# Dense scores in a hybrid encoder layer: the second products of two key tiles, 64 rows deep, in the two halves of the rows

## The chip, the cores and the metric

The kernel runs on one core of one Trainium2 chip. The core has a matrix engine (TensorE, PE in the profile, with its loads of weights as PEld), a vector engine (VectorE, DVE), an engine for functions (ScalarE, ACT), a general engine (GpSimd, POOL) and an engine that only issues transfers (SyncE, SP). SBUF, the memory that all of them read, has 128 rows (partitions). A matmul multiplies weights and moving data that both lie along the rows, adds up over the rows, and writes into a bank of the accumulator memory (PSUM). How many rows take part is the depth of the product. The metric is the device time of one execution in microseconds (us); lower is better.

## The reference, cut to what matters

One encoder layer on 1024 tokens with a model width of 1024. An input projection feeds two groups of attention heads: group A is dense, 8 query heads that share 2 key heads, with a norm on queries and keys and a rotary embedding; group B looks through dilated windows. Then come an output projection and a feed-forward part with a convolution. The change touches the dense scores of group A alone:

```python
def global_gqa_attention(q, k, v):
    b, s = q.shape[0], q.shape[1]
    nb = s // Q_BLOCK
    qg = q.reshape(b, nb, Q_BLOCK, N_KV_A, GQA_GROUP, HEAD_DIM).transpose(1, 0, 2, 3, 4, 5)
    scale = HEAD_DIM ** -0.5

    def block(qb):
        sc = jnp.einsum('bqkgd,bskd->bkgqs', qb, k, preferred_element_type=jnp.float32) * scale
        p = jax.nn.softmax(sc, axis=-1)
        return jnp.einsum('bkgqs,bskd->bqkgd', p.astype(v.dtype), v)
```

A head has 64 dimensions, so a score is a product of depth 64. All is float32.

## The kernel before

**Split numbers.** PE takes float32 in a rounded form (fp32r). To keep the precision, the kernel splits a value x into a high part (x rounded to fp32r) and a low part (x less the high part, rounded). A product of queries q and keys k is then high x high + high x low + low x high. With depth 64 two of the three fit into one product of depth 128. The tile that starts at R_K2A holds, for each tile of 128 keys, the low parts of k in rows 0 to 63 and the high parts in rows 64 to 127. The queries' tile q2 (R_Q2A) holds the high parts of q in rows 0 to 63 and the low parts in rows 64 to 127. Their product gives low x high and high x low. A second tile, R_KHA, holds the high parts of k in rows 0 to 63 and zeros below, and its product with q2 gives high x high. The two products add up in one bank.

**The dense stage.** The function a_main_bounded does one group: one block of 128 queries, 4 heads that share a key head, so 512 columns. There are 16 groups. A group has 8 tiles of 128 keys, taken in 4 steps j of two tiles u = 0, 1. In a step PE makes the scores of both tiles in two neighbouring banks (L773 and L774, twice each), ACT takes the exponential of both at once (L779), ACT or DVE rounds it to the high part (L783, L781), and DVE makes the low part (L784). Three steps later PE multiplies with the values (L757, six matmuls of 512 columns for a step). At a group's end DVE copies the result (L767), PE transposes it (L762), and DVE divides by the sum (L803, L804).

**Preparation.** a_prep makes q2 for the next group while the present one runs. Its step nat splits the queries (L665 on ACT, L666 on DVE); its step first transposes them on PE (L192, in the helper tr_r) and lets ACT copy them to q2 (L687). q2 has two buffers, which the groups use in turn. A table in the main loop, plan, tells behind which of the eight key tiles of a group the next of these steps is taken: (0, 1, 0, 0, 1, 0, 0, 0) takes nat behind tile 1 and first behind tile 4, that is in steps j = 0 and j = 2.

**Other work in the stage.** Sums, norms and rotary turns that are left over from the projection are dealt out over the first groups (on POOL L530 and L304, on DVE L537 and L540 among others), and a tick, a small copy (L1323, L558), ties each to the group that it is to run in. Later groups carry the norms of group B's queries, and parts of the next stage's preparation (L849 and L850 split its keys, L838 and L839 its values). Transfers within SBUF go through POOL's queue: k_ready makes R_KHA in that way with four transfers (L354), and the next stage does the same (L880). The engines' queues are in order; a scheduler sets the order of each from the program, so a step can stand earlier or later than the code reads.

Of the kernel before, what the change touches and what calls it, by code (L numbers as in the profile page):

```python
# [45 lines left out]
R_K2A = 16384  # L46
R_KHA = R_K2A + 2048
R_W = R_KHA + 6144
# [26 lines left out]
R_QLN = R_XT + 1024  # L75
R_Q2A = R_XT + 2048
R_QLA = R_XT + 3072
R_PH = R_XT + 4096
R_PL = R_XT + 6144
R_VB = R_XT + 8192  # L80
# [2 lines left out]
R_VA = R_XT + 9248  # L83
R_PHB = (R_PH, R_PH + 1024, R_XT + 1024, R_XT + 13824)
R_PLB = (R_PL, R_PL + 1024, R_XT + 3072, R_XT + 14848)
# [51 lines left out]
def tile_encoder_layer(ctx, tc, x, w_in, gains, outg, norm1_g, norm2_g, w_out, w_up, conv_w, conv_b,  # L137
# [14 lines left out]
    def emit(bounded):  # L152
# [3 lines left out]
        gp = nc.gpsimd  # L156
        mm = nc.tensor.matmul
# [5 lines left out]
        def r(off, n):  # L163
            return bigr[:, off:off + n]
# [20 lines left out]
        def bank(i, n=512, o=0):  # L185
            return PS[:, 512 * i + o:512 * i + o + n]
# [26 lines left out]
        def next_tr():  # L213
            trb[0] ^= 1
            return 4 + trb[0]
# [8 lines left out]
        def qab(tt):  # L224
            return O_QAB + 1024 * tt
# [424 lines left out]
        def p_slots():  # L650
            i = p_n[0]
            p_n[0] += 1
            return p_ring[i % len(p_ring)], R_PH + 512 * (i % 4), R_PL + 512 * (i % 4)

        def q_nat(src, stride, eng, n, o, qln=R_QLN):

            q = fp(src, [stride, n], [1, 64])
            act(rp(R_QD + o, [128, n], [64, 2], [1, 64]), fp(src, [stride, n], [0, 2], [1, 64]), AF.Copy)
            eng.tensor_tensor(rp(qln + o, [128, n], [1, 64]), q, rfp(R_QD + o, [128, n], [1, 64]), op=OP.subtract)


        def q_pair(src, stride, eng, n, o):

            q = fp(src, [stride, n], [1, 64])
            act(rp(R_QD + o, [128, n], [1, 64]), q, AF.Copy)  # L665
            eng.tensor_tensor(rp(R_QD + 64 + o, [128, n], [1, 64]), q, rfp(R_QD + o, [128, n], [1, 64]), op=OP.subtract)  # L666

        def grp(g):
            b, kv = divmod(g, 2)
            return (4 * (g // 8) + g % 4, g // 4 % 2) if bounded else (b, kv)  # L670

        def a_prep(g):
            b, kv = grp(g)
            o = 512 * (g % 2)
            q2 = R_Q2A + 512 * (g % 2)
            ql = R_QLA + 512 * (g % 2)

            def nat():
                if bounded:
                    return q_pair(qab(b) + 256 * kv, 64, vec, 4, o)  # L680
                q_nat(qab(b) + 256 * kv, 64, vec, 4, o)

            def first():
                t = next_tr()
                for i in range(4):
                    tr_r(t, i, r(R_QD + o + 128 * i, 128))
                act(r(q2, 512), bank(t), AF.Copy)  # L687

            def mx(i):
                for hf in range(2):  # L690
                    b = hf
                    mm(bank(b), r(q2 + 128 * i, 128), r(R_K2A + 1024 * kv + 512 * hf, 512), start=True, stop=True)
                    vec.tensor_reduce(f(SM_MC + 8 * hf + i, 1), bank(b), axis=AX.X, op=OP.max)

            def last():
                vec.tensor_tensor(rp(R_QLN + 512 * kv + 64, [128, 4]), f(SM_MC, 4), f(SM_MC + 8, 4), op=OP.max)
                t = next_tr()
                for i in range(4):
                    tr_r(t, i, r(R_QLN + 128 * (4 * kv + i), 128))
                act(r(ql, 512), bank(t), AF.Copy)  # L700

            if bounded:
                return [nat, first]
            return [nat, first] + [lambda i=i: mx(i) for i in range(4)] + [last]

        def a_main(g, prep, tail, late, plan, late_plan):
# [4 lines left out]
            q2 = R_Q2A + 512 * (g % 2)  # L711
            ql = R_QLA + 512 * (g % 2)
            ob = 6 + g % 2
# [29 lines left out]
        def a_main_bounded(g, prep, tail, late, plan, late_plan):  # L743

            b, kv = grp(g)
            b2, kv2 = grp(max(g - 2, 0))
            q2 = R_Q2A + 512 * (g % 2)
            ob = 6 + g % 2
            slots = {}

            def pv(j):
                ph, pl = slots[j]
                for u in range(2):
                    kt = 2 * j + u
                    v = R_VA + 132 * kt + 66 * kv
                    for i, (w, p) in enumerate(((v, ph), (v + 1056, ph), (v, pl))):
                        mm(bank(ob)[0:66], r(w, 66), r(p + 512 * u, 512), start=(kt == 0 and i == 0), stop=(kt == 7 and i == 2))  # L757

            def o_turn():
                t = next_tr()  # L760
                for i in range(4):
                    nc.tensor.transpose(bank(t, 66, 128 * i), f(F_OT + 128 * i, 128)[0:66], f(O_IDF, 66)[0:66])  # L762
                o_norm(t, 128, qab(b) + 256 * kv, ([64, 4], [1, 64]))

            def last():
                pv(3)
                vec.tensor_copy(f(F_OT, 512)[0:66], bank(ob)[0:66])  # L767

            for j in range(4):
                st = 2 * (j % 2)  # L770
                for u in range(2):
                    kt = 2 * j + u
                    mm(bank(st + u), r(R_K2A + 1024 * kv + 128 * kt, 128), r(q2, 512), start=True, stop=False)  # L773
                    mm(bank(st + u), r(R_KHA + 1024 * kv + 128 * kt, 128), r(q2, 512), start=False, stop=True)  # L774
                n = pairs[0]
                pairs[0] += 1
                p, ph, pl = F_PB[n % 3], R_PHB[j], R_PLB[j]
                slots[j] = ph, pl
                act(f(p, 1024), bank(st, 1024), AF.Exp)  # L779
                if j == 1:  # L780
                    vec.tensor_copy(r(ph, 1024), f(p, 1024))  # L781
                else:
                    act(r(ph, 1024), f(p, 1024), AF.Copy)  # L783
                vec.tensor_tensor(r(pl, 1024), f(p, 1024), rf(ph, 1024), op=OP.subtract)  # L784
                for kt in (2 * j, 2 * j + 1):
                    take(prep, plan[kt])
                    take(late, late_plan[kt])
                    now = f(qab(b2) + 256 * kv2, 1) if 0 < kt < 7 and g > 1 else \
                        rf(R_Q2A + 512 * ((g + (kt == 7)) % 2), 1)
                    for step in spread.pop((g, kt), []):  # L790
                        step(now)
                step = tail.pop(0) if tail else None
                if step:
                    step()
                if j > 2:
                    pv(j - 3)

            behind, turn[:] = turn[:], [o_turn]
            return [lambda: [t() for t in [lambda: pv(1)] + behind], lambda: pv(2), last, o_turn if g == 15 else None]
# [189 lines left out]
        def b_p_bounded(h, i):  # L989
            ta, tb = F_TEE[h % 2]  # L990
            st, p = 2 * (i % 2), F_PD[i]
            if not fine(i):
                vec.tensor_tensor(fp(p, [512, 2], [256, 2], [1, 256]), pp(512 * st, [512, 2], [256, 2], [1, 256]),
                                  fp(tb, [0, 2], [128, 2], [1, 256]), op=OP.mult)
                return
            ph, pl = R_PH + 512 * i, R_PL + 512 * i
            vec.tensor_tensor(fp(p, [256, 4], [64, 4], [1, 64]), pp(512 * st, [256, 4], [64, 4], [1, 64]),
# [4 lines left out]
        def b_pv_bounded(h, i):  # L1002
            if fine(i):
                ph, pl = R_PH + 512 * i, R_PL + 512 * i
                for u in range(4):
# [344 lines left out]
        for g in range(16):  # L1350

            prep += a_prep(g + 1) if g < 15 else []
            if g == 14:
                prep += [lambda: b_split(0)] + sum(sum(b_prep(0), []), [])
            plan = {14: (1, 1, 0, 1, 0, 1, 1, 0), 15: (1, 1, 0, 1, 0, 0, 0, 0)}.get(g, (0, 1, 0, 0, 1, 0, 0, 0)) if bounded else {14: (1, 1, 1, 1, 1, 2, 2, 2), 15: (2, 2, 2, 2, 1, 1, 1, 1)}.get(
                g, (1, 1, 1, 1, 1, 1, 1, 0))
            tail = a_main(g, prep, tail, late, plan, (0, 2, 2, 2, 1, 1, 1, 1))
            if g == 7:
                if not bounded:
                    dma(f(F_CNT, 384), cnt)  # L1360
                if not bounded:
                    gp.memset(fp(F_VCN + 64, [66, 8]), 1.0)
                    load_vc(0)
            if g in (4, 7):
                wo_load(g // 7)
            if g == 9:
                load_tee(0, 0)
                load_tee(0, 1)
                load_tmx(1)
            if g == 11:  # L1370
                load_k(0)
            if g == 13:
                load_k(1)
            if g == 10 and bounded:
                load_v(0)
            if g == (12 if bounded else 5):
                v_split(R_VB, F_VBN)
                load_v(1)
            if g > 3 and fills:
                b, kv = grp(g - 2 if bounded else g - 1)  # L1380
                fills.pop(0)(qab(b) + 256 * kv)
# [411 lines left out]
        for m in range(2, len(order)):  # L1793
            j, n = order[m]
# [111 lines left out]
```

## Time and profile before

| | us |
|---|---|
| median of 3 runs (lowest, highest) | 1220.58 (1219.28, 1222.5) |
| the profiled execution | 1221.38 |
| its span in the profile | 1219.6 |
| the dense stage, 16 groups, 207.5 to 364.6 | 157.1 |

The profile shows one execution. A row of the timeline gives the start, the length and what ran; several instructions of the same kind are merged, with their number behind an x. A row of a group of instructions gives the number, the busy time, the mean length in ns, and the idle time before. A matmul's shape stands as rows*columns of the weights, then the moving data. The ends of matmuls are modelled, so their starts are the safer reading. Weights are loaded by an instruction of their own, which can run beside a matmul.

### The profile page before, as it was taken

The page shows a single profiled execution, that of the slowest core. Times are in us where ns is not written, and L with a number is a line of the kernel's source. Part 1 is how long each engine was busy: PE and PEld are TensorE (multiplying, and loading weights), DVE is VectorE, ACT ScalarE, POOL GpSimd, SP SyncE. Part 2 cuts the span into 40 slices and gives each one's busy share as a digit, 9 for nine tenths or more (in the row PEclk, how much of TensorE's full clock was granted, in tenths as well). Part 3 has the DMA queues.
Part 4 walks back from the last instruction along what each step waited for, and adds up shares of the span by engine and source line. Part 5 has one row for each costly group of instructions (what it writes and reads, how often), then busy time and mean ns, then how long its engine had stood idle before and what let it go on. Part 6 is the DMA issues. An engine that isn't in the chain of part 4 may idle for free.

```text
span 1219.6 us, 17814 instructions
## 1 busy us (share of the span) xinstructions
PE 1191.7 (98%) x6615; PEld 1007.2 (83%) x6615; DVE 998.0 (82%) x1324; ACT 674.1 (55%) x976; POOL 398.4 (33%) x307
## 2 busy tenths in 40 slices
PE   7999999999999999999999999999999999999998
PEld 7999999666669997888788888877888788888886
DVE  5988687989988878666999999999999997876673
ACT  7856455889887767436544444445444453543431
POOL 1710122230024530010465666557575644000000
PEclk9999999999999999999999999999999999999999
DMA  8036301020015655232132232322332257977872
GB/s 281 25 103 154 108 18 42 1 57 18 1 30 125 153 117 173 89 102 95 61 112 95 87 113 97 111 95 87 113 112 100 83 184 252 338 239 243 291 233 85
DMA packets 121565, 147.00 MB, mean 121 GB/s; under 512 B 51137, under 2 KB 79617, under 8 KB 121473
## 3 DMA queue, kind: packets, MB, share of 16 engines
q1 hardware_dynamic: 119329, 140.05, 35.9%
q0 software_dynamic: 2144, 5.77, 2.2%
q8 instruction: 53, 0.87, 0.3%
q14 instruction: 39, 0.32, 0.1%
HBM read 107.25 MB, written 33.82 MB: 116 GB/s over the span
## 4 chain that ended last, share of the span: by engine, by line
PE 68%; DVE 17%; issue 5%; ACT 4%; DMA 3%; POOL 1%; SPq 0%; DVEq 0%; ACTq 0%; POOLq 0%
DVE bigf L1603 7%; PE ps L1570 7%; PE ps L1572 6%; PE ps L1571 6%; PE ps L757 6%; PE ps L1704 6%; PE ps L1703 6%; PE ps L1702 6%; DVE bigf L1574 3%; PE ps L1125 2%; PE ps L1126 2%; PE ps L1124 2%; PE ps L434 2%; PE ps L435 2%; PE ps L773 2%
## 5 line engine op out<-in xcount | busy, mean ns | idle before, releaser
L1570 PE MATMUL ps<-bigr 128*128 128x512 f32 x616 | 241.0, 392 | 6.3 <-DVE bigf L1574 5.8
L1571 PE MATMUL ps<-bigr 128*128 128x512 f32 x616 | 239.7, 389 | 0.0
L1572 PE MATMUL ps<-bigr 128*128 128x512 f32 x616 | 239.7, 389 | 0.0
L1603 DVE SCALAR_TENSOR_TENSOR bigf<-bigf 128x768 f32<-128x768 f32 (+1 forms) x176 | 178.7, 1073 | 26.5 <-ACT bigf L1601 26.4
L1553 ACT ACTIVATE bigr<-bigf 128x512 fp32r<-128x512 f32 x154 | 93.2, 625 | 139.5 <-POOL bigf L1545 70.2
L1682 ACT ACTIVATE bigr<-bigf 128x1024 fp32r<-128x1024 f32 (+1 forms) x99 | 83.7, 867 | 115.8 <-PE ps L1704 67.6
L1570 PEld LDWEIGHTS ps<-bigr 128*128 128x128 f32 x616 | 115.6, 188 | 35.0 <-DVE bigf L1574 9.2
L1572 PEld LDWEIGHTS ps<-bigr 128*128 128x128 f32 x616 | 115.6, 188 | 24.1
L1571 PEld LDWEIGHTS ps<-bigr 128*128 128x128 f32 x616 | 115.7, 188 | 23.7
L434 PE MATMUL ps<-bigr 128*128 128x256 f32 x448 | 127.3, 285 | 1.2 <-ACT bigf L310 1.2
L1554 DVE TENSOR_TENSOR bigr<-bigf,bigr 128x512 fp32r<-128x512 f32 x112 | 125.2, 1135 | 3.2 <-ACT bigr L1553 2.5
L435 PE MATMUL ps<-bigr 128*128 128x256 f32 x448 | 126.9, 283 | 0.6 <-DVE bigr L418 0.6
L436 PE MATMUL ps<-bigr 128*128 128x256 f32 x448 | 126.7, 283 | 0.0
L1702 PE MATMUL ps<-bigr 128*128 128x512 f32 x308 | 119.8, 389 | 0.0
L1703 PE MATMUL ps<-bigr 128*128 128x512 f32 x308 | 119.8, 389 | 0.0
L1704 PE MATMUL ps<-bigr 128*128 128x512 f32 x308 | 119.8, 389 | 0.0
L1683 DVE TENSOR_TENSOR bigr<-bigf,bigr 128x1024 fp32r<-128x1024 f32 (+1 forms) x99 | 97.6, 1005 | 24.8 <-ACT bigr L1682 21.4
L757 PE MATMUL ps<-bigr 128*66 128x512 f32 x384 | 99.9, 394 | 0.0
L434 PEld LDWEIGHTS ps<-bigr 128*128 128x128 f32 x448 | 85.8, 192 | 1.8 <-ACT bigf L310 1.5
L435 PEld LDWEIGHTS ps<-bigr 128*128 128x128 f32 x448 | 85.9, 192 | 0.8 <-DVE bigr L418 0.8
L784 DVE TENSOR_TENSOR bigr<-bigf,bigr 128x1024 fp32r<-128x1024 f32 x64 | 80.8, 1269 | 6.4 <-ACT bigr L783 5.7
L436 PEld LDWEIGHTS ps<-bigr 128*128 128x128 f32 x448 | 85.9, 192 | 0.0
(231 smaller groups left out, 2508.8 us busy)
## 6 DMA issues: line engine op xcount, KB each, us to landing
bigf<-w_down SPq DMA_DIRECT2D x99, 256.0 KB, 4.3
bigf<-w_up SPq DMA_DIRECT2D x44, 512.0 KB, 3.6
bigf<-gscr SPq DMA_DIRECT2D x77, 256.0 KB, 4.3
gscr<-bigf SPq DMA_DIRECT2D x31, 512.0 KB, 2.6
bigf<-w_in SPq DMA_DIRECT2D x8, 1024.0 KB, 5.4
bigf<-x SPq DMA_DIRECT2D x15, 512.0 KB, 7.0
bigf<-w_out SPq DMA_DIRECT2D x8, 512.0 KB, 3.9
bigr<-bigr POOLq DMA_DIRECT2D x16, 256.0 KB, 3.8
```

Of the source, the lines that this page charges most:

```text
L434: mm(o, ah, wh, start=(k == 0 and t % 2 == 0 and n != 2), stop=False, skip_group_check=True)
L435: mm(o, ah, wl, start=False, stop=False, skip_group_check=True)
L436: mm(o, al, wh, start=False, stop=(k == 3), skip_group_check=True)
L757: mm(bank(ob)[0:66], r(w, 66), r(p + 512 * u, 512), start=(kt == 0 and i == 0), stop=(kt == 7 and i == 2))
L1554: (gp if n in (2, 4) and m > 3 else vec).tensor_tensor(rp(o + 512, [128, 4], [1, 128]), src, rfp(o, [128, 4], [1, 128]), op=OP.subtract)
L1570: mm(bank(b), wh, th, start=(k == 0 and n in (1, 5, 6, 7)), stop=False, skip_group_check=True)
L1571: mm(bank(b), wh, tl, start=False, stop=False, skip_group_check=True)
L1572: mm(bank(b), wl, th, start=False, stop=(k == 3), skip_group_check=True)
L1603: vec.scalar_tensor_tensor(f(a + o, n), f(i + d, n), w_, f(a + o, n), op0=OP.mult, op1=OP.add)
L1702: mm(o, ah, r(d, 512), start=(q == 0 and n in (1, 5, 2)), stop=False, skip_group_check=True)
L1703: mm(o, ah, r(d + 1024, 512), start=False, stop=False, skip_group_check=True)
L1704: mm(o, al, r(d, 512), start=False, stop=(q == NQ - 1), skip_group_check=True)
```

## The change

Three things are edited, in the dense stage alone.

The second products of a step's two key tiles, which gave high x high at a depth of 128 with zeros in half of the rows, are now 64 rows deep. That of tile u = 0 reads rows 0 to 63 of R_KHA and of q2. That of tile u = 1 reads rows 64 to 127 of R_K2A, where the high parts of its keys lie already, and rows 64 to 127 of a new tile, R_Q3A. The two stand one behind the other, after the two first products. No tile's depth was 64 in the program before.

R_Q3A takes a copy of the queries' high parts, moved from rows 0 to 63 to rows 64 to 127. A transfer on POOL's queue makes it for each group, in the step first behind the copy on ACT. It has two buffers, as q2 has.

The table plan takes first one step earlier, behind tile 2 (j = 1), and in group 14 its entries move.

```diff
+R_Q3A = R_W + 6144
...
                 act(r(q2, 512), bank(t), AF.Copy)
+                if bounded:
+                    gp.dma_start(r(R_Q3A + 512 * (g % 2), 512)[64:128], r(q2, 512)[0:64])
...
                 st = 2 * (j % 2)
+                k2, kh = [o + 1024 * kv + 256 * j for o in (R_K2A, R_KHA)]
                 for u in range(2):
-                    kt = 2 * j + u
-                    mm(bank(st + u), r(R_K2A + 1024 * kv + 128 * kt, 128), r(q2, 512), start=True, stop=False)
-                    mm(bank(st + u), r(R_KHA + 1024 * kv + 128 * kt, 128), r(q2, 512), start=False, stop=True)
+                    mm(bank(st + u), r(k2 + 128 * u, 128), r(q2, 512), start=True, stop=False)
+                mm(bank(st), r(kh, 128)[0:64], r(q2, 512)[0:64], start=False, stop=True)
+                mm(bank(st + 1), r(k2 + 128, 128)[64:128], r(R_Q3A + 512 * (g % 2), 512)[64:128], start=False, stop=True)
...
-            plan = {14: (1, 1, 0, 1, 0, 1, 1, 0), 15: (1, 1, 0, 1, 0, 0, 0, 0)}.get(g, (0, 1, 0, 0, 1, 0, 0, 0)) if bounded else
+            plan = {14: (1, 0, 1, 0, 1, 1, 1, 0), 15: (1, 1, 0, 1, 0, 0, 0, 0)}.get(g, (0, 1, 1, 0, 0, 0, 0, 0)) if bounded else
```

Lines of the changed kernel have other numbers: the first products are L776, the second L777 (u = 0) and L778 (u = 1), the products with the values L760, the transposes of queries L193, of results L765, the copy on ACT L688, the new transfer L690.

PE's queue in one group of the dense stage, from its step j = 1, before:

```order
L773 MATMUL ps<-bigr 128x512
L774 MATMUL ps<-bigr 128x512
L773 MATMUL ps<-bigr 128x512
L774 MATMUL ps<-bigr 128x512
L757 MATMUL ps<-bigr 66x512 x6
L773 MATMUL ps<-bigr 128x512
L774 MATMUL ps<-bigr 128x512
L773 MATMUL ps<-bigr 128x512
L774 MATMUL ps<-bigr 128x512
L192 MATMUL ps<-bigr 128x128 x4
L757 MATMUL ps<-bigr 66x512 x6
```

And the same place now:

```order
L776 MATMUL ps<-bigr 128x512 x2
L777 MATMUL ps<-bigr 128x512
L778 MATMUL ps<-bigr 128x512
L193 MATMUL ps<-bigr 128x128 x4
L760 MATMUL ps<-bigr 66x512 x6
L776 MATMUL ps<-bigr 128x512 x2
L777 MATMUL ps<-bigr 128x512
L778 MATMUL ps<-bigr 128x512
L760 MATMUL ps<-bigr 66x512 x6
```

The two second products now stand together between the two first ones and the six with the values, and the transposes of the next group's queries (L193) stand one step earlier.

POOL's queue from k_ready's transfers through the dense stage, before:

```order
L354 DMA bigr<-bigr 64x2x256 x4
L530 TENSOR_TENSOR bigf<-bigf 128x512
L304 TENSOR_TENSOR bigf<-bigf 128x8x16 x8
L530 TENSOR_TENSOR bigf<-bigf 128x512
L304 TENSOR_TENSOR bigf<-bigf 128x8x16 x8
L530 TENSOR_TENSOR bigf<-bigf 128x512
L304 TENSOR_TENSOR bigf<-bigf 128x8x16 x8
L1452 MEMSET bigf 128x8
L850 TENSOR_TENSOR bigr<-bigf,bigr 128x8x64
L839 TENSOR_TENSOR bigr<-bigf,bigr 128x8x64
```

And now, from the first turns on (L531 and L305 are the table and the turns, L854 and L843 the splits of keys and values):

```order
L305 TENSOR_TENSOR bigf<-bigf 128x8x16 x8
L690 DMA bigr<-bigr 64x512 x3
L531 TENSOR_TENSOR bigf<-bigf 128x512
L305 TENSOR_TENSOR bigf<-bigf 128x8x16 x8
L690 DMA bigr<-bigr 64x512
L531 TENSOR_TENSOR bigf<-bigf 128x512
L305 TENSOR_TENSOR bigf<-bigf 128x8x16 x8
L1456 MEMSET bigf 128x8
L690 DMA bigr<-bigr 64x512
L854 TENSOR_TENSOR bigr<-bigf,bigr 128x8x64
L690 DMA bigr<-bigr 64x512
L843 TENSOR_TENSOR bigr<-bigf,bigr 128x8x64
```

The new transfers stand among the turns and the splits: one ahead of this piece, those of groups 1 to 3 ahead of the second table, that of group 4 ahead of the third, those of groups 5 and 6 behind the last turns, and the other nine behind the split of the values.

More of the change, by code (lines that the diff above doesn't have):

```diff
@@ L1354, in emit @@
                 prep += [lambda: b_split(0)] + sum(sum(b_prep(0), []), [])
-            plan = {14: (1, 1, 0, 1, 0, 1, 1, 0), 15: (1, 1, 0, 1, 0, 0, 0, 0)}.get(g, (0, 1, 0, 0, 1, 0, 0, 0)) if bounded else {14: (1, 1, 1, 1, 1, 2, 2, 2), 15: (2, 2, 2, 2, 1, 1, 1, 1)}.get(
+            plan = {14: (1, 0, 1, 0, 1, 1, 1, 0), 15: (1, 1, 0, 1, 0, 0, 0, 0)}.get(g, (0, 1, 1, 0, 0, 0, 0, 0)) if bounded else {14: (1, 1, 1, 1, 1, 2, 2, 2), 15: (2, 2, 2, 2, 1, 1, 1, 1)}.get(
                 g, (1, 1, 1, 1, 1, 1, 1, 0))
```

## The prediction

> **What bounds the kernel now.** I read the page's busy times first, then the groups of instructions, then the timeline of one group of the dense stage, then the same stage cut at the starts of its sixteen groups.
>
> ```profile
> span 1219.6 us, 17814 instructions
> PE 1191.7 (98%) x6615; PEld 1007.2 (83%) x6615; DVE 998.0 (82%) x1324; ACT 674.1 (55%) x976; POOL 398.4 (33%) x307
> ...
> L773 PE MATMUL ps<-bigr 128*128 128x512 f32 x128 | 51.7, 404 | 0.3 <-ACT bigr L687 0.3
> ...
> L774 PE MATMUL ps<-bigr 128*128 128x512 f32 x128 | 50.3, 393 | 0.0
> ```
>
> L773 and L774 are the two products of the dense scores, 128 of each, and only this stage is edited. A record of 393 ns is not what a matmul costs here. The timeline of PE in one group shows the cost:
>
> ```profile
> 289.07 0.40 PE L774 MATMUL ps<-bigr 128*128 128x512 f32 x1
> 289.30 0.39 PE L773 MATMUL ps<-bigr 128*128 128x512 f32 x1
> 289.53 0.39 PE L774 MATMUL ps<-bigr 128*128 128x512 f32 x1
> ...
> 294.68 1.56 PE L757 MATMUL ps<-bigr 128*66 128x512 f32 x6
> 296.08 0.41 PE L762 MATMUL ps<-bigf 66*128 66x66 f32 x4
> 296.30 0.48 PE L773 MATMUL ps<-bigr 128*128 128x512 f32 x1
> ```
>
> The second column is a record's length, but the starts are 0.23 us apart (289.07, 289.30, 289.53). So 0.23 us is the slot of a matmul, and 0.39 - 0.23 = 0.16 us of each record lies under the next one: two are in flight at once. The weights are loaded ahead, in the slot before:
>
> ```profile
> 288.84 0.19 PEld L774 LDWEIGHTS ps<-bigr 128*128 128x128 f32 x1
> 289.07 0.19 PEld L773 LDWEIGHTS ps<-bigr 128*128 128x128 f32 x1
> ```
>
> The load for the matmul that starts at 289.30 begins at 289.07, so its 0.19 us are hidden. A group has 40 slots, 16 for scores and 24 for L757: 40 x 0.23 = 9.2 us. Two sets of four transposes bring it near 9.8 us. Here is the stage by group (columns: the stretch, its length, then PE, PEld, DVE, ACT and POOL busy, with instructions in brackets, the granted clock, and DMA):
>
> ```profile
> 207.53:213.01 5.48, 5.21 (x29) 3.91 (x27) 3.90 (x5) 4.64 (x7) 0.00 (x0) 1.00 0.00 0
> 213.01:223.31 10.30, 10.30 (x44) 6.93 (x45) 10.30 (x13) 9.55 (x12) 0.00 (x0) 1.00 0.00 0
> 223.31:233.16 9.85, 9.85 (x49) 6.83 (x48) 8.44 (x13) 7.97 (x11) 4.07 (x4) 1.00 0.01 2
> 233.16:243.00 9.84, 9.84 (x50) 6.84 (x48) 9.28 (x13) 7.86 (x10) 3.69 (x6) 1.00 0.00 1
> 243.00:252.87 9.87, 9.87 (x50) 6.85 (x49) 7.37 (x14) 7.89 (x10) 7.25 (x10) 1.00 0.19 47
> 252.87:264.24 11.37, 10.07 (x50) 6.76 (x48) 10.68 (x16) 8.45 (x11) 3.10 (x1) 1.00 0.36 88
> 264.24:274.07 9.83, 9.83 (x50) 6.86 (x49) 9.35 (x17) 9.19 (x13) 1.39 (x1) 1.00 0.11 27
> 274.07:283.93 9.86, 9.86 (x50) 6.79 (x48) 9.80 (x16) 9.76 (x12) 0.00 (x0) 1.00 0.19 53
> 283.93:293.77 9.84, 9.84 (x49) 6.83 (x49) 9.54 (x19) 8.72 (x11) 0.00 (x0) 1.00 0.01 2
> 293.77:303.89 10.12, 10.12 (x50) 6.79 (x48) 9.55 (x16) 9.52 (x13) 0.00 (x0) 1.00 0.00 0
> 303.89:313.61 9.72, 9.72 (x48) 6.81 (x48) 8.92 (x16) 9.68 (x12) 0.00 (x0) 1.00 0.01 2
> 313.61:323.46 9.85, 9.85 (x49) 6.83 (x48) 9.57 (x17) 8.01 (x10) 0.00 (x0) 1.00 0.00 1
> 323.46:333.31 9.85, 9.85 (x49) 6.84 (x48) 9.61 (x15) 7.88 (x9) 0.00 (x0) 1.00 0.00 0
> 333.31:343.13 9.82, 9.82 (x49) 6.86 (x48) 9.72 (x18) 8.32 (x12) 0.00 (x0) 1.00 0.12 28
> 343.13:354.66 11.53, 10.68 (x58) 7.45 (x56) 8.67 (x12) 9.98 (x14) 1.42 (x1) 1.00 0.00 1
> 354.66:364.60 9.94, 9.94 (x53) 7.04 (x52) 7.45 (x8) 9.47 (x13) 4.68 (x5) 1.00 0.28 54
> sum 157.07, PE 154.66 PEld 107.21 DVE 142.13 ACT 136.89 POOL 25.60; mean PE 9.67 PEld 6.70 DVE 8.88 ACT 8.56 POOL 1.60
> ```
>
> PE fills 154.7 of 157.1 us, at full clock (1.00). So the stage is bound by PE, slot after slot, and what a slot costs more or less goes into the time. But DVE (142.1) and ACT (136.9) are close behind, and in the group at 274.07 they are busy 9.80 and 9.76 us of 9.86. A slower PE costs nearly in full, a faster one is soon caught by the other two.
>
> **The change, part by part.** The sum is made against the profiled execution, 1221.4 us (span 1219.6 and 1.8 around it), which is 0.8 above the median of the runs, 1220.6.
>
> *The slots.* Four full-depth slots per step become two full-depth ones and two of 64 rows. The two of 64 rows read different halves of the rows and write different banks, so they can share a slot. No row here shows two matmuls in one slot: the pair costs between 0.23 us (together) and 0.46 (one after the other). I take 0.23, since neither needs anything of the other. With 16 groups of 4 steps, that is 64 pairs x 0.23 = 14.7 us off PE at most.
>
> *The change of depth.* PE now goes from 128 rows to 64 and back in each step, 128 changes in all. No dense slot of before does that. Two rows bound it. From below, L762 above: its 66-row transposes start at 296.08, and the sixth L757 before it started about 294.68 + 5 x 0.23 = 295.83, so another kind of matmul came in after 0.25 us, a slot as usual: cost 0. From above, the only matmul of fewer than 64 rows:
>
> ```profile
> 6.48 0.18 PEld L593 LDWEIGHTS ps<-bigf 8*128 8x128 f32 x1 [0.33 <-issue]
> 6.48 0.27 PE L593 MATMUL ps<-bigf 8*128 8x8 f32 x1
> ```
>
> Its load of weights and its matmul start together, so nothing was loaded ahead. If a change waits until PE is empty and only then loads weights, it costs 0.16 + 0.19 = 0.35 us. I take the step between the ends, 0.16: the matmul in flight ends before the next depth begins, but weights are still loaded ahead. It lies next to the middle of 0 and 0.35. Two changes are then 0.32 us against 0.23 saved, so a step loses 0.32 - 0.23 = 0.09 to 0.10 us, and 64 steps lose about 6.1 us. The ends are -14.7 us on PE and 64 x (0.70 - 0.23) = +30 us.
>
> The Trainium skill speaks against this change at this point: "TensorEngine Tiling (Array Packing)", section "Tiling Modes", says that changing the tiling mode, not just the tile, drains the TensorE. It gives no time for that; by it the sum is on the losing side, +6 us or more, and without it on the winning side. No row of this profile shows a drain, so the trace neither agrees nor disagrees.
>
> *The copy.* Sixteen transfers of 64 x 512 go into POOL's queue. Nearest are the four of L354, as large and within SBUF:
>
> ```profile
> L354 POOL DMA_DIRECT2D bigr<-bigr x4: 578/587/813, 189.2 to 196.7; - x4
> ...
> DMA to landing us min/median/max: 2.3/2.6/3.8
> ```
>
> POOL pays 0.59 us for each, 9.4 us in all, and has 157.1 - 25.6 us free in the stage; that is its cover. PE needs the copy for the fourth product of a group. The transposes of the next group's queries move up one step (ten slots, about 2.4 us), which pays for most of the 2.6 us. Three places are tight. In the first group there is no slack:
>
> ```profile
> 212.35 0.60 ACT L687 ACTIVATE bigr<-ps 128x512 fp32r<-128x512 f32 x1
> ...
> 213.01 0.50 PE L773 MATMUL ps<-bigr 128*128 128x512 f32 x1 [0.27 <-ACT bigr L687]
> ```
>
> L687 moves up by one exponential here and ends near 212.0; the group's first product follows it at once, and its copy lands near 212.0 + 2.6 = 214.6 (from the issue), against a need three slots in, at 212.1 + 0.7 = 212.8. PE would wait 1.8 us, but DVE is busy for all of the next group (10.30 of 10.30), so part is hidden: between 0 and 2 us, I take 1. In the group at 252.87 the transfer stands in POOL's queue behind the turns:
>
> ```profile
> 244.02 2.49 POOL bigf L530
> ...
> 246.58 4.73 POOL bigf L304 x8
> ...
> 251.33 1.23 DVE bigf L537
> ```
>
> This is the chain of waits: POOL is done at 251.3, the copy lands at 253.9, needed at 253.6. That group idles 11.37 - 10.07 = 1.3 us on this chain anyway, so I take nothing. Last, b_split's L850 and v_split's L839 stand between the later transfers; they keep their places, and the copies of groups 6 and 7 wait behind them, with the 2.4 us in hand: 0, at most 1.
>
> *The order.* The moved transposes (L192) are the same work earlier, but they need the split of the queries (L666 on DVE) one step sooner.
>
> ```profile
> 285.85 0.41 DVE L666 TENSOR_TENSOR bigr<-bigf,bigr 128x256 fp32r<-128x256 f32 x1
> ...
> 289.76 0.45 PE L192 MATMUL ps<-bigr 128*128 128x128 f32 x4
> ```
>
> Here it is done 3.5 us ahead (289.76 - 286.26), more than the 2.4 that they move. The other moves on ACT and DVE change places, not work: 0.
>
> *Sum.* +6.1 (depth) + 1 (first copy) - 0.8 (the groups at 252.87 and 343.13 idle 1.3 and 0.85 us on other engines, which covers their 0.4 each) = +6.3 us. From the median: 1220.6 + 6.3 = **1227 us**.
>
> **The rivals.** *A change of depth costs nothing* (faster). Then PE has 0.92 us less to do in a group. What of it can be had is what DVE and ACT leave: for each group the lesser of 0.92 and its length less the busier of DVE and ACT. In the rows above from the third on that is 0.92, 0.56, 0.92, 0.69, 0.48, 0.06, 0.30, 0.57, 0.04, 0.28, 0.24, 0.10, 0.92, 0.47, and nothing in the first two (they wait for L687 and DVE): 6.5 us, so 1214. It ends at 1217 if the chain through POOL keeps the groups at 243.00 and 252.87 (1.6 us) and the first copy is late, and at 1211 if a lead in one group helps the next. For it speaks L762, which slots in without a gap; against it, that L762 keeps the full depth. It decides below 0.11 us a change, where the two changes cost the slot saved. The Trainium skill, "TensorE: Matmul & The Clock Gate", section "Part 3: Packing small matmuls — row/col tiling", says that tiles in different row groups run at once, some 4 ns apart; by that rule alone this rival is the result, and no row here shows it.
>
> *PE empties and the loading is exposed as well* (slower still): 0.35 us a change, 64 x 0.47 = 30 us, less about 2 in the groups that idle: 1248. For it speaks L593; against it, that L593 may have waited for its own data.
>
> *The pair doesn't run together and a change costs nothing*: four slots as before, 1221, with late copies up to 1223. The records would then show the pair 0.23 us apart.
>
> **How the numbers follow.** Forecast 0.43 (its own range 1223 to 1232: 0.14 to 0.2 us a change, first copy 0 to 2), no cost of depth 0.35, exposed loading 0.13, nothing gained 0.09. Within 0.3% (3.7 us) two times cannot be told apart. Slower: 0.40 of the forecast, 0.13, and 0.03 of the last, 0.56. Faster: 0.33 of the first rival. Same: 0.03 + 0.02 + 0.06 = 0.11. The range 1211 to 1246 takes in the first rival and the near part of the second, and leaves out some 0.12.
>
> **What would show it.** In the timeline of PE, the second half's product starts within a few hundredths of the first half's; the first half's product starts 0.39 us (not 0.23) after the last full one, and the first L757 behind the pair 0.39 after it. A group then takes about 10.2 us, and DVE's share of the stage falls. If the group shrinks to 9.5 or less with DVE near 100%, the first rival holds; if the weights' loads of the pair start only after the last full product ends, the second. Waits of PE for the copy should show in the group at 213 alone. The forecast is wrong above all if the array changes its depth as it goes.

## The result, and the profile after

| | before | changed |
|---|---|---|
| median (us) | 1220.92 | 1229.07 |
| lowest to highest | 1219.28 to 1222.5 | 1228.02 to 1229.21 |
| runs | 4 | 4 |
| span of the profiled execution | 1219.6 | 1227.1 |
| dense stage in it, first score to the next stage's first product | 157.2 | 164.5 |

The changed kernel is slower: ratio 1.0062, 95% interval 1.005 to 1.0075. The forecast was 1227. Of the 7.5 us between the spans, 7.3 stand in the dense stage. One execution of two_steps_half below (1461.6 us) and one of the kernel before beside it (1468.4) ran at a granted clock of 0.75 and are left out of the ratios.

The page's busy times and the groups of instructions on PE in the changed kernel (L776 is the first product, L777 and L778 the pair of 64 rows, L760 the products with the values):

```profile
span 1227.1 us, 17854 instructions
PE 1201.3 (98%) x6615; PEld 992.8 (81%) x6615; DVE 998.9 (81%) x1324; ACT 677.0 (55%) x976; POOL 406.8 (33%) x323
...
L760 PE MATMUL ps<-bigr 128*66 128x512 f32 x384 | 102.8, 400 | 0.0
L776 PE MATMUL ps<-bigr 128*128 128x512 f32 x128 | 41.5, 405 | 0.0
L777 PE MATMUL ps<-bigr 64*128 64x512 f32 x64 | 31.7, 496 | 0.0
L778 PE MATMUL ps<-bigr 64*128 64x512 f32 x64 | 31.7, 496 | 0.0
```

PE has as many matmuls as before, and the records of the pair are 496 ns long against 393 for the product that they replace. The timeline of PE shows where a step's time goes:

```profile
287.30 0.63 PE L776 MATMUL ps<-bigr 128*128 128x512 f32 x2
287.86 0.50 PE L777 MATMUL ps<-bigr 64*128 64x512 f32 x1
287.86 0.50 PE L778 MATMUL ps<-bigr 64*128 64x512 f32 x1
288.29 1.60 PE L760 MATMUL ps<-bigr 128*66 128x512 f32 x6
```

And a stretch a little later, in which the second of the two L776 has a row of its own, with the loads of weights:

```profile
290.26 0.40 PE L776 MATMUL ps<-bigr 128*128 128x512 f32 x1
...
290.59 0.18 PEld L777 LDWEIGHTS ps<-bigr 64*128 64x128 f32 x1 [0.37 <-issue]
290.59 0.49 PE L777 MATMUL ps<-bigr 64*128 64x512 f32 x1
290.59 0.18 PEld L778 LDWEIGHTS ps<-bigr 64*128 64x128 f32 x1
290.60 0.50 PE L778 MATMUL ps<-bigr 64*128 64x512 f32 x1
```

Three things are to be seen. The pair does share a slot: its two products start together. The pair starts 0.33 us after the last full product (290.59 - 290.26), where a slot is 0.23. And its weights begin to load only then, at the same moment as the products' records, after 0.37 us in which the loader waited for nothing that the profile names ("issue"). In a plain step of the kernel before, each load ran under the slot ahead of it.

The way back reads alike: L760 follows the pair after 0.43 us (288.29 - 287.86), and six of them last 1.60 us where six lasted 1.54 to 1.56.

The dense stage by group (the columns as in the prediction; four of the sixteen, and the sum):

```profile
213.64:224.92 11.28, 11.28 (x44) 5.96 (x45) 10.69 (x14) 9.99 (x13) 0.51 (x1) 1.00 0.12 23
...
255.84:266.60 10.76, 10.54 (x50) 5.71 (x48) 10.72 (x15) 9.10 (x12) 4.83 (x3) 1.00 0.42 103
...
287.30:297.68 10.38, 10.38 (x49) 5.80 (x48) 8.85 (x17) 9.42 (x11) 0.51 (x1) 1.00 0.07 14
...
349.29:361.88 12.59, 11.25 (x57) 6.41 (x56) 8.06 (x11) 9.86 (x14) 3.15 (x2) 1.00 0.06 10
...
sum 164.48, PE 162.88 PEld 90.78 DVE 143.71 ACT 139.88 POOL 33.97; mean PE 10.18 PEld 5.67 DVE 8.98 ACT 8.74 POOL 2.12
```

A plain group takes 10.3 to 10.4 us instead of 9.85, and DVE and ACT do the same work as before in more time. PE bounds the stage more than it did.

### The profile page after: what moved, and what is told of

The parts are those of the page before. It is cut to its first block, busy times and chain, and to the rows that moved or that the text cites. A ratio compares the mean times of both kernels' runs of the same rounds, so it can differ in the third digit from the quotient of the medians.

```text
span 1227.1 us, 17854 instructions
## 1 busy us (share of the span) xinstructions
PE 1201.3 (98%) x6615; PEld 992.8 (81%) x6615; DVE 998.9 (81%) x1324; ACT 677.0 (55%) x976; POOL 406.8 (33%) x323
## 4 chain that ended last, share of the span: by engine, by line
PE 57%; DVE 19%; issue 13%; ACT 4%; DMA 4%; POOL 2%; SPq 0%; DVEq 0%; POOLq 0%; ACTq 0%
DVE bigf L1607 7%; PE ps L1574 7%; PE ps L1576 6%; PE ps L1575 6%; PE ps L1706 6%; PE ps L1707 6%; PE ps L1708 6%; DVE bigf L1578 2%; PE ps L1128 2%; PE ps L1130 2%; PE ps L1129 2%; PE ps L760 2%; PE ps L990 2%; DVE bigr L1558 2%; PE ps L1023 2%
## 5 line engine op out<-in xcount | busy, mean ns | idle before, releaser
L1687 DVE TENSOR_TENSOR bigr<-bigf,bigr 128x1024 fp32r<-128x1024 f32 (+1 forms) x99 | 96.6, 995 | 23.9 <-ACT bigr L1686 20.6
L760 PE MATMUL ps<-bigr 128*66 128x512 f32 x384 | 102.8, 400 | 0.0
```

## The experiments

Six kernels ran, four on one chip and two on another, each beside the kernel before. The theory: each change between 128 and 64 rows stops PE for a fixed time, and two changes cost more than the slot that the pair saves. The diffs are against the changed kernel where nothing else is said. The rivals: the copy and the moved steps cost the time; the 64-row products are slow in themselves or don't share a slot; the cost goes by the pair and not by the change.

### copy_full_depth: the copy and the order, without the depth

```diff
-                mm(bank(st), r(kh, 128)[0:64], r(q2, 512)[0:64], start=False, stop=True)
-                mm(bank(st + 1), r(k2 + 128, 128)[64:128], r(R_Q3A + 512 * (g % 2), 512)[64:128], start=False, stop=True)
+                for u in range(2):
+                    mm(bank(st + u), r(kh + 128 * u, 128), r(q2, 512), start=False, stop=True)
```

> The changed kernel with its copy, its table and its order, but the two second products at the full depth of 128 again (the copy is made and not read). If the change of depth is the cost, this stands near the kernel before: 1221 to 1222.5 us, and a dense group takes 9.8 us again. If the copy and the moved steps are the cost, it stands near the changed kernel, 1228 to 1229, with groups of 10.3.

Measured: 1222.25 us against 1221.15 before, ratio 1.0008 (0.9999 to 1.0017). The whole dense stage in one window, and a step of it:

```profile
207.31:365.69 158.38, 154.76 (x757) 107.44 (x756) 142.90 (x212) 138.82 (x166) 35.79 (x42) 1.00 0.15 32
```

```profile
291.56 0.62 PE L776 MATMUL ps<-bigr 128*128 128x512 f32 x2
292.01 0.62 PE L778 MATMUL ps<-bigr 128*128 128x512 f32 x2
292.46 1.53 PE L760 MATMUL ps<-bigr 128*66 128x512 f32 x6
```

Four slots from 291.56 to 292.46, 0.23 each again. The sixteen transfers, the moved transposes and the changed orders of ACT and DVE cost the stage 1.2 us (158.4 against 157.2), and the change of depth the rest. The 1.2 us are all idle time of PE (158.38 - 154.76 = 3.6 us, where the kernel before has 2.4); over the executions the interval takes in no difference at all. What this run can't hold is a wait of PE for the copy, since nothing reads it.

### same_half: both products of 64 rows in the lower half, no copy

```diff
-                if bounded:
-                    gp.dma_start(r(R_Q3A + 512 * (g % 2), 512)[64:128], r(q2, 512)[0:64])
...
-                mm(bank(st), r(kh, 128)[0:64], r(q2, 512)[0:64], start=False, stop=True)
-                mm(bank(st + 1), r(k2 + 128, 128)[64:128], r(R_Q3A + 512 * (g % 2), 512)[64:128], start=False, stop=True)
+                for u in range(2):
+                    mm(bank(st + u), r(kh + 128 * u, 128)[0:64], r(q2, 512)[0:64], start=False, stop=True)
```

> Both second products 64 rows deep, but both in the lower half of the rows, and no copy. If the two halves share a slot in the changed kernel and each step pays 0.35 us for two changes of depth, this one pays the 0.35 without the shared slot: 64 x 0.35 = 22 us over the kernel before, 1242 (1239 to 1245), and the second half-depth product starts 0.23 us after the first. If the halves share nothing, or 64-row products are slow in themselves, it stands with the changed kernel at 1229.

Measured: 1241.78 us, ratio 1.0169 (1.0154 to 1.0184). The timeline of a step:

```profile
290.20 0.63 PE L774 MATMUL ps<-bigr 128*128 128x512 f32 x2
290.76 0.73 PE L776 MATMUL ps<-bigr 64*128 64x512 f32 x2
291.42 1.62 PE L758 MATMUL ps<-bigr 128*66 128x512 f32 x6
```

The two half-depth products now take 0.66 us from start to start of what follows (290.76 to 291.42), against 0.43 for the pair in two halves: the difference is one slot of 0.23. So the halves do share a slot in the changed kernel, and this sharing, less what the copy costs, is worth 1241.8 - 1229.1 = 12.7 us. The cost of the depth is what eats it: without the sharing, 20.6 us over the kernel before, 0.32 us a step. One expectation failed: the second product starts 0.34 us after the first (0.73 less a record of 0.39), not 0.23.

```profile
207.33:385.14 177.81, 176.91 (x756) 97.88 (x755) 143.84 (x212) 140.98 (x166) 26.10 (x27) 1.00 0.07 18
```

In the dense stage PE was busy for 22.2 us more than before (176.91 - 154.66), which is 0.35 us a step, and its idle time fell from 2.4 to 0.9 us. So the two changes cost PE 0.35, as expected; 0.32 is what is left of it.

### half_then_full: one half-depth product, and another neighbour behind it

```diff
-                for u in range(2):
-                    mm(bank(st + u), r(kh + 128 * u, 128)[0:64], r(q2, 512)[0:64], start=False, stop=True)
+                mm(bank(st), r(kh, 128)[0:64], r(q2, 512)[0:64], start=False, stop=True)
+                mm(bank(st + 1), r(kh + 128, 128), r(q2, 512), start=False, stop=True)
```

(The diff is against same_half.)

> As same_half, without copy, but the second of the two second products at full depth: two changes in a step, one 64-row product, and the change back is now to 128 columns of weights, not 66. If weights load with nothing over them at each change, this costs 64 x 0.05 = 3.3 us more than same_half: 1245. If weights are loaded ahead, as the prediction took, the two are alike, 1242. If the cost goes by the number of 64-row products, it halves: 1231.

Measured: 1244.66 us, ratio 1.0196 (1.0179 to 1.0213). It stands 24.0 us above the kernel before that ran beside it, same_half 20.6 above its own: 3.4 us between them, where 3.3 were expected of loads that are not ahead. The timeline of a step (L775 is the one of 64 rows):

```profile
291.24 0.62 PE L774 MATMUL ps<-bigr 128*128 128x512 f32 x2
291.79 0.49 PE L775 MATMUL ps<-bigr 64*128 64x512 f32 x1
292.21 0.50 PE L776 MATMUL ps<-bigr 128*128 128x512 f32 x1
292.55 1.55 PE L758 MATMUL ps<-bigr 128*66 128x512 f32 x6
```

The full product behind the change now has the long record (0.50) and holds its successor off for 0.34 us (292.55 - 292.21); the six behind it are back at 1.55. So whichever matmul comes first after a change carries the load of its weights: about 0.11 us for 128 columns (0.34 - 0.23), 0.05 us for 66 (1.60 - 1.55). Half as many 64-row products didn't halve the cost.

### four_changes: the pair taken apart

```diff
-                for u in range(2):
-                    mm(bank(st + u), r(k2 + 128 * u, 128), r(q2, 512), start=True, stop=False)
+                mm(bank(st), r(k2, 128), r(q2, 512), start=True, stop=False)
                 mm(bank(st), r(kh, 128)[0:64], r(q2, 512)[0:64], start=False, stop=True)
+                mm(bank(st + 1), r(k2 + 128, 128), r(q2, 512), start=True, stop=False)
                 mm(bank(st + 1), r(k2 + 128, 128)[64:128], r(R_Q3A + 512 * (g % 2), 512)[64:128], start=False, stop=True)
```

> The changed kernel with the pair taken apart: first product of tile 0, its second product (64 rows, lower half), first product of tile 1, its second product (64 rows, upper half). Four changes of depth in a step in place of two, and no shared slot. In the trace of the changed kernel a change to 64 rows costs 0.20 us (the array empties, 0.10, and 128 columns of weights load with nothing over them, 0.11), a change back to 66 columns of weights 0.145, to 128 columns 0.20: 0.75 a step, 64 x 0.75 = 48 us, with the copy about 1268 (1262 to 1272). If the cost were one by the pair or by the 64-row product, it would be the changed kernel and the lost slots, 1229 + 15 = 1244.

Measured: 1265.34 us, ratio 1.037 (1.0352 to 1.0387). The timeline of a step (L775 and L777 full, L776 and L778 of 64 rows):

```profile
291.98 0.40 PE L775 MATMUL ps<-bigr 128*128 128x512 f32 x1
292.31 0.50 PE L776 MATMUL ps<-bigr 64*128 64x512 f32 x1
292.74 0.50 PE L777 MATMUL ps<-bigr 128*128 128x512 f32 x1
293.17 0.50 PE L778 MATMUL ps<-bigr 64*128 64x512 f32 x1
293.60 1.60 PE L760 MATMUL ps<-bigr 128*66 128x512 f32 x6
```

Each product that stands between two changes takes 0.43 us, a slot and 0.20. Twice as many changes, 44.7 us over the kernel before (which took 1220.68 beside it) instead of 20.6 in same_half, which has no shared slot either. The copy, which same_half lacks, is in the 44.7; in copy_full_depth it came to 1.1. The cost goes by the change.

### two_steps_half and two_steps_full: half as many changes

Both make the scores of the steps j and j + 1 together when j is even (only the added lines are shown).

```diff
+                for i in (j, j + 1) if j % 2 == 0 else ():
+                    for u in range(2):
+                        mm(bank(2 * (i % 2) + u), r(R_K2A + 1024 * kv + 256 * i + 128 * u, 128), r(q2, 512), start=True, stop=False)
+                for i in (j, j + 1) if j % 2 == 0 else ():
+                    k2, kh = [o + 1024 * kv + 256 * i for o in (R_K2A, R_KHA)]
+                    t = 2 * (i % 2)
+                    mm(bank(t), r(kh, 128)[0:64], r(q2, 512)[0:64], start=False, stop=True)
+                    mm(bank(t + 1), r(k2 + 128, 128)[64:128], r(R_Q3A + 512 * (g % 2), 512)[64:128], start=False, stop=True)
```

In two_steps_full the second loop makes the two second products at full depth, and the copy is left out.

> The changed kernel with the scores of two steps made together: four first products, then the two pairs of 64 rows, so 64 changes of depth in place of 128. If the cost is by the change of depth, a pair of steps pays 0.35 us and saves 2 x 0.23: 32 x 0.11 = 3.5 us less than the same order at full depth (two_steps_full), near 1217.5. If the cost is by the pair of products, it stays at 1229. If DVE and ACT can't take the scores in bursts, both kernels of two steps are slower alike.

> The control for two_steps_half: the scores of two steps together, all at a depth of 128, no copy. PE has the same slots as before, so 1221 if ACT and DVE keep up with scores in bursts of eight slots; up to 1226 if they don't.

Measured: two_steps_half 1225.64 us, ratio 1.0034 (1.0023 to 1.0045); two_steps_full 1224.83 us, ratio 1.0028 (1.0017 to 1.0039). I expected two_steps_half to be 3.5 us below two_steps_full, at 1217.5; neither came. Where the four first products stand together, the step does what was worked out (timeline of two_steps_half; L780 and L781 are the pairs):

```profile
293.91 0.86 PE L776 MATMUL ps<-bigr 128*128 128x512 f32 x3
294.70 0.50 PE L780 MATMUL ps<-bigr 64*128 64x512 f32 x1
294.70 0.50 PE L781 MATMUL ps<-bigr 64*128 64x512 f32 x1
295.04 0.39 PE L780 MATMUL ps<-bigr 64*128 64x512 f32 x1
295.04 0.39 PE L781 MATMUL ps<-bigr 64*128 64x512 f32 x1
295.37 0.45 PE L760 MATMUL ps<-bigr 128*66 128x512 f32 x1
```

The second pair has records of 0.39 again, since its weights loaded under the first pair: between pairs of the same depth there is no stop. From 293.91 to 295.37 these are 1.46 us, where seven slots would be 1.61; 0.05 of the difference goes into the first L760, so some 0.1 us is gained here. But the stage shows three things that I had left out. The first two stand in the waits of the loader:

```profile
PEld ps L780 <- issue: 14.0, 39, 0.4
...
PEld ps L781 <- DMA bigr<-bigr: 2.6, 1, 2.6
...
PEld ps L781 <- issue: 1.1, 3, 0.4
```

There were 42 changes to 64 rows (39 and 3), not 32, because the scheduler kept some steps apart, and 60 of the 64 pairs shared a slot in the trace. That makes 42 x 0.35 = 14.7 us against 60 x 0.23 = 13.8 saved, so 0.9 us lost in place of 3.5 gained. And one group's copy came late: POOL sent it at 254.89, behind its turns, and PE stood still for 2.3 us, until 257.21. The prediction took nothing for this copy in the changed kernel, and PE has no wait for it there.

The third is the order itself: two_steps_full loses 3.7 us with no change of depth. In its stage PE idles 2.4 us more than before (161.05 - 156.23 = 4.8), above all where the scores wait for ACT to free their banks:

```profile
PEld ps L774 <- ACT bigf L782: 5.0, 8, 2.4
```

The rest goes with the clock. The stretch behind its longest wait, and two behind the late copy in two_steps_half (the clock is the third figure from the end):

```profile
267.77:272.20 4.43, 4.43 (x18) 3.01 (x19) 2.23 (x5) 4.19 (x5) 1.29 (x1) 0.63 0.20 46
```

```profile
257.20:262.00 4.80, 4.79 (x18) 2.97 (x19) 4.00 (x6) 3.00 (x3) 0.00 (x0) 0.50 0.48 109
262.00:266.00 4.00, 4.00 (x16) 2.24 (x16) 3.67 (x7) 1.79 (x4) 2.10 (x2) 0.80 0.20 37
```

PE was granted 0.63, 0.50 and 0.80 of its clock there, where the dense stages of the other kernels stand at 1.00. I estimate the loss as the length times the missing share: 4.43 x 0.37 = 1.6 us in two_steps_full, 4.80 x 0.50 + 4.00 x 0.20 = 3.2 us in two_steps_half.

With these the stages add up. That of two_steps_full is 3.8 us longer than before (161.05 against 157.23): 2.4 of idle time and 1.6 of clock. That of two_steps_half is 5.6 longer (162.85): 1.6 of idle time (162.85 - 158.86 = 4.0), 3.2 of clock and 0.9 of depth.

Both falls come with a wait of PE of 2.0 us or more; the waits of 1.3 and 1.6 us in the stages of the kernel before and of copy_full_depth have none behind them. The length of the wait alone doesn't decide, since outside its dense stage the changed kernel has a clock of 0.50 behind a wait of 1.2 us (470.2 to 473.4), and the kernel before has 1.00 behind one as long (at 463.2). What sets the fall off was not tried, and it need not be in every execution: the two of two_steps_half with a mean clock of 1.000 took 1222.9 and 1224.1 us, the five others in the ratio 1225.1 to 1227.0.

So the price by the change holds, but an order with fewer changes made PE wait, and that cost more than the changes brought. No version beat the kernel before.

## Why the prediction was right, and where it was not

**PE bounds the stage, and a slot costs 0.23 us.** Right: copy_full_depth shows the same slots with everything else of the change in place.

**The pair shares a slot.** Right. Its products start within 0.01 us of each other in 63 of the 64 steps, and same_half is 12.7 us slower for having them in one half. By the rule of the Trainium skill, "TensorE: Matmul & The Clock Gate", section "Part 3: Packing small matmuls — row/col tiling", tiles in different row groups start some 4 ns apart; the trace agrees (290.59 and 290.60).

**The change of depth, 0.16 us each.** Near in size, wrong in kind. The prediction took it that PE waits until the matmul in flight has ended, 0.39 us after its start, and that weights are still loaded ahead. Measured, PE waits less, and weights are not loaded ahead:

| part of a step | us | from |
|---|---|---|
| wait before the pair | 0.10 | 0.33 - 0.23 |
| load of the pair's weights, uncovered | 0.11 | 0.34 - 0.23 (same_half; half_then_full has the same for 128 rows) |
| wait behind the pair | 0.09 | 0.43 - 0.23 - 0.11 |
| load of the next weights (66 columns), uncovered | 0.05 | 1.60 - 1.55 |
| both changes | 0.35 | |
| the shared slot | -0.23 | |
| a step | +0.12 | |

So a change costs 0.17 us on average, against 0.16 in the forecast; the step that failed is "weights are still loaded ahead". Two errors met: a shorter wait, and a load that was taken for covered. That the number came so near is luck in part. 64 steps x 0.12 = 7.7 us, where the forecast had 6.1. Of the signs that the prediction named, the pair's common start and the falling share of DVE came (142.1 of 157.1 us before, 143.7 of 164.5 now). The 0.39 us at both changes came as 0.33 and 0.43, and the loads that begin only behind the wait were the sign of the second rival.

The row L762, taken as the bound from below, says nothing of a change to 64 rows: its products of 66 rows still follow a full one after 0.23 us in the changed kernel, so they are no such change. L593 did show a load that starts with its matmul. What such a load costs stood in the trace before, in the row behind one that the prediction shows:

```profile
213.34 0.39 PE L774 MATMUL ps<-bigr 128*128 128x512 f32 x1
```

The L773 ahead of it, at 213.01, had waited for ACT, and its load started with it (213.00). L774 follows after 0.33 us, a slot and 0.10, with no change of depth near. This row prices a load that isn't ahead at 0.10 us and not at the 0.19 of its record, and its long record, 0.50, is the one that the pair has now.

The rule of the Trainium skill that spoke against the change, "TensorEngine Tiling (Array Packing)", section "Tiling Modes", is that changing the tiling mode drains the TensorE. The trace agrees so far that the pair's load waits 0.37 us on "issue" and the pair starts 0.10 us later than a slot; whether the array is empty by then no record shows, since the pair starts 0.07 us before the modelled end of the last full product (290.26 + 0.40).

Every kernel here that changes depth shows the longer record behind the change, and copy_full_depth, which doesn't change it, has slots of 0.23 in its plain steps.

**The copy.** Right in its cover, wrong in its one cost. POOL paid 0.51 us (the median) for a transfer, under its idle time. The prediction let PE wait 1.8 us for the first one and counted 1 us. The scheduler had instead put five products with the values between the halves of that pair:

```profile
214.30 0.50 PE L777 MATMUL ps<-bigr 64*128 64x512 f32 x1
214.74 1.37 PE L760 MATMUL ps<-bigr 128*66 128x512 f32 x5
216.03 0.50 PE L778 MATMUL ps<-bigr 64*128 64x512 f32 x1
216.46 1.37 PE L760 MATMUL ps<-bigr 128*66 128x512 f32 x5
```

The last of the five starts near 215.70 and L778 0.33 us later, so nothing but the change of depth holds it. That took the wait away, at the price of two more changes of depth and the shared slot, 0.35 + 0.23 = 0.6 us. I had compared the two orders of PE in a plain group only; this stood in the order, one group further up.

**The groups that idle.** Half right. The group at 252.87 idled 1.3 us before and 0.2 after (10.76 - 10.54), so it covered the change, and more than the 0.4 counted. The group at 343.13 covered nothing: its idle time grew from 0.85 to 1.34 us (12.59 - 11.25). PE waits there for POOL's split of the queries of the next stage, which took 1.42 us before and 2.24 after:

```profile
356.21 2.24 POOL L667 TENSOR_TENSOR bigr<-bigf,bigr 128x512 fp32r<-128x512 f32 x1
```

It took 2.24 us in copy_full_depth and 2.25 in same_half and half_then_full, which have no copy, so it doesn't come with the transfers. All four have the moved steps (the table's entry for group 14); why the split takes longer there stays open.

**The sum.** PE's busy time in the stage grew by 8.2 us (162.88 - 154.66). The prices above give 65 x 0.35 - 63 x 0.23 = 8.3, with the two extra changes and the lost slot of the first group: 7.7 for the depth and 0.6 in place of the 1 for the copy. PE's idle time fell by 0.8 us, from 2.4 (157.07 - 154.66) to 1.6 (164.48 - 162.88). The forecast has 0.8 here too, but from two groups that would cover 0.4 each; it came as 1.1 and 0.2 less in two groups and 0.5 more in a third, and that the sums meet is luck. In all that is 7.4 us, against 7.5 between the spans and 8.2 between the medians. The forecast was 6.3, and the term that was too small is the depth.

**The rivals.** That a change of depth costs nothing fell in every run that has one. That PE empties and the load is exposed as well was right in kind, but it was priced with the full records, 0.16 + 0.19, where the trace has 0.10 + 0.11: the part of a record that holds PE up is shorter than the record. That the pair doesn't run together fell with same_half.

## What to carry to other kernels

Matmuls of half the depth in the two halves of the rows do run at once, but each change between this and full depth stops PE for a wait and for one uncovered load of weights, here 0.35 us for the two, so one pair of 512 columns (0.23 us saved) doesn't pay. Two in a row (0.46 saved) gain some 0.1 us by these prices and in the one stretch shown, but no kernel here gained by them. Before counting on more of them in a row, make the same order at full depth: the control here lost 3.7 us for its order alone, by waits of PE and by the lower clock that came with one of them. And where a scheduler sets the queue, compare the orders in the first groups and the last, not only in a plain one.

## What was not expected of the hardware

In plain steps loads of weights are ahead by a slot as long as the depth stays, and not across a change of it: all 42 changes to 64 rows in two_steps_half have a load that starts with its matmul, while the load of the second of two pairs in a row is ahead. The uncovered part goes with the columns of the weights, 0.11 us for 128 and 0.05 for 66, though the load's own record is 0.18 us for 64 rows and 128 columns: a record is longer than the time for which it holds up the next. And a single wait of PE of some 2 us can cost more than itself: in both kernels of two steps a stretch at half the clock came with it (0.50 for 4.8 us in two_steps_half).
